# Rotation products of an SSM state stage that read PSUM instead of a ScalarE copy in SBUF

## The chip, the cores and the metric

One Trainium2 chip, one of its cores. The metric is the device time of one execution in microseconds (us), the median of three runs. Engines are named as the profile names them: PE is TensorE, DVE is VectorE, ACT is ScalarE, POOL is GpSimd, SP issues DMAs.

## The reference

One decoding step of a four-layer trunk of width 1024, in float32. It takes 272 prompt tokens (16 learned ones and 256 given) and 8 x 4 sample tokens, 304 in all. Layers 0 and 3 mix tokens with an S5 state-space model, layer 1 with pooling, layer 2 with attention; a convolutional FFN follows each. What the change touches is the state-space mixer:

```python
    a_bar = jnp.exp(lam * dt)
    b_bar = ((a_bar - 1.0) / lam)[:, :, None] * b_mat
    bu = jnp.einsum('gpc,blgc->blgp', b_bar, ug)            # complex
    bu = bu.at[:, 0].add(a_bar * h0)
    _, h = lax.associative_scan(_ssm_combine, (a_seq, bu), axis=1)
    y = jnp.real(jnp.einsum('gcp,blgp->blgc', c_mat, h)) + d_skip * uf
    z = jax.nn.gelu(y) @ w_glu
    out = z[..., :D_MODEL] * jax.nn.sigmoid(z[..., D_MODEL:])
```

## The kernel before, in words

The sequence is cut into chunks of four tokens: 68 of the prompt, 8 of the samples. Channels come in eight blocks of 128, d = 0 to 7. The complex recurrence over chunks is done in rotated coordinates, so that a real scan is enough: the inputs of the scan are multiplied by a cosine and a sine table (PT, `cs` and `sn`), scanned with the real decay R, and rotated back.

`ssm()` runs its steps in an order written as a string, `ORDER_FIRST` for layer 0 and `ORDER` for layer 3; a letter is a kind of step, the digit its block. The ones that matter here:

- i, `inputs(d)`: brings the block's tokens into the layout U by transposes on TensorE (L1062, L1067) and copies on ScalarE (u, U). In layer 3 VectorE first makes xn (L1059).
- s, `states(d)`: TensorE multiplies U by M1 (L1093), 8 small matmuls for the real part (r = 0) and 8 for the imaginary one (r = 1), each r into a PSUM bank of its own. ScalarE copies the prompt's 4 x 68 columns of a bank to E (L1095, 128x272) and the samples' 4 x 8 to Es (L1096, 128x32). VectorE then forms four products of 128x272: for each half b of the prompt E times cs (L1101) and E with r reversed times sn (L1102). One add and one subtract put them back into E (L1103, L1104). Two scans follow (L1111), the second takes over the end of the first (L1114 to L1117), then the rotation back (t3 on L1118, t4_ on L1119) and X (L1121).
- v, `outmat(d)`: GpSimd builds V from Cn and A (va on L1133, vb on L1134, then V on L1138: two instructions on VectorE for r = 0, two on GpSimd for r = 1).
- o, `outputs(d)`: TensorE multiplies U and X by m and V (L1155, L1157), ScalarE takes the GELU into z (L1159), TensorE transposes it (L1163), and ScalarE and VectorE split it into a high and a low part (zhi L1166, zlo L1167).
- g, `glu0`: groups of the GLU's matrix product, three matmuls for each product of split numbers (L248 to L250; the one with zlo is L249). Their weights are split by ScalarE (hi, L208) and by VectorE or GpSimd (lo, L211).

PSUM has eight banks; `bank()` hands out the next one as soon as its last reader is done. A list scheduler that simulates a timeline sets each engine's order from these steps, and each engine then runs its instructions strictly in that order. Each of the engines therefore waits at its own first unready instruction.

Of the kernel before, what the change touches and what calls it, by code (L numbers as in the profile page):

```python
# [9 lines left out]
F32 = mybir.dt.float32  # L10
F32R = mybir.dt.float32r
I32 = mybir.dt.int32
AF = mybir.ActivationFunctionType
ALU = mybir.AluOpType
# [8 lines left out]
KP = NP // 4  # L23
KB = KP // 2
# [22 lines left out]
def bc(ap, pos, n):  # L47

    a = ap.unsqueeze(pos)
    shape = list(a.shape)  # L50
    shape[pos] = n
    return a.broadcast_to(shape)
# [8 lines left out]
class Trunk:  # L61
# [925 lines left out]
    def ssm(self, j, l, first):  # L987
        nc, I, O = self.nc, self.I, self.O
        v, g = nc.vector, nc.gpsimd
        with self.tc.tile_pool(name=f"ssm{l}", bufs=1) as sp:  # L990
# [89 lines left out]
            def states(d):  # L1080


                qt, i0 = d // 2, d % 2 * 4
                qs = slice(4 * d, 4 * d + 4)
                M1 = self.M1[qt]
                R, E = R2[d % 2], E2[d % 2]
                nc.scalar.activation(R[:, :, :, 1:], bc(bc(self.r4[:, qs], 2, KB), 1, 2), AF.Copy)
                for r in range(2):
                    pt = self.bank()
                    for i in range(4):  # L1090
                        for h in range(2):
                            hs = slice(h * 64, h * 64 + 64)
                            nc.tensor.matmul(pt[hs, i * NK:(i + 1) * NK], M1[hs, r, i0 + i], U[d][hs, i], start=True, stop=True)  # L1093
                    pv = pt[:, :4 * NK].rearrange("p (q k) -> p q k", k=NK)
                    nc.scalar.activation(E[:, :, r, :, 1:], pv[:, :, :KP].rearrange("p q (b k) -> p b q k", b=2), AF.Copy)  # L1095
                    nc.scalar.activation(Es[:, r, qs], pv[:, :, KP:], AF.Copy)  # L1096
                cs, sn = (bc(self.PT[qt][:, i, i0:i0 + 4], 1, 2) for i in range(2))
                t1 = sp.tile([128, 2, 2, 4, KB], F32, name="t1", tag="t1", bufs=1)
                t2 = sp.tile([128, 2, 2, 4, KB], F32, name="t2", tag="t2", bufs=1)
                for b in range(2):  # L1100
                    v.tensor_tensor(t1[:, b], E[:, b, :, :, 1:], cs, ALU.mult)  # L1101
                    v.tensor_tensor(t2[:, b], E[:, b, ::-1, :, 1:], sn, ALU.mult)  # L1102
                v.tensor_tensor(E[:, :, 0, :, 1:], t1[:, :, 0], t2[:, :, 0], ALU.add)  # L1103
                v.tensor_tensor(E[:, :, 1, :, 1:], t1[:, :, 1], t2[:, :, 1], ALU.subtract)  # L1104
                x = X[d] = X3[d % 3]
                t3 = sp.tile([128, 2, 2, 4, KB], F32, name="t3", tag="t1", bufs=1)
                t4_ = sp.tile([128, 2, 2, 4, KB], F32, name="t4_", tag="t2", bufs=1)
                e1 = sp.tile([128, 2, 2, 4], F32, name="e1", tag="e1")
                for b in range(2):
                    e = E[:, b].rearrange("p r q k -> p (r q k)")  # L1110
                    v.tensor_tensor_scan(e, R.rearrange("p r q k -> p (r q k)"), e, 0.0, ALU.mult, ALU.add)  # L1111
                    if b == 0:

                        v.tensor_tensor(e1[:, 0], E[:, 0, :, :, KB], cs[:, :, :, KB - 1], ALU.mult)  # L1114
                        v.tensor_tensor(e1[:, 1], E[:, 0, ::-1, :, KB], sn[:, :, :, KB - 1], ALU.mult)
                        v.tensor_tensor(E[:, 1, 0, :, 0], e1[:, 0, 0], e1[:, 1, 0], ALU.subtract)
                        v.tensor_tensor(E[:, 1, 1, :, 0], e1[:, 0, 1], e1[:, 1, 1], ALU.add)  # L1117
                    v.tensor_tensor(t3[:, b], E[:, b, :, :, 1:], cs, ALU.mult)  # L1118
                    v.tensor_tensor(t4_[:, b], E[:, b, ::-1, :, 1:], sn, ALU.mult)  # L1119
                for r, op in ((0, ALU.subtract), (1, ALU.add)):  # L1120
                    last_s[d] = v.tensor_tensor(x[:, r, :, 1:KP + 1].rearrange("p q (b k) -> p b q k", b=2), t3[:, :, r], t4_[:, :, r], op)  # L1121
                nc.scalar.activation(fin[:, :, 8, qs], x[:, :, :, KP], AF.Copy)
                self.behind_act = nc.scalar.activation(x[:, :, :, KP:], h0[:, :, :, qs].rearrange("p r b q -> p r q b"), AF.Copy)
# [84 lines left out]
            def lift():  # L1208
                self.cap = 1 << 30

            steps = {"i": inputs, "r": residual, "w": self.ssm_w, "m": self.ssm_m, "k": self.ssm_k, "p": lambda q: self.ssm_phase(*((0, 1, v), (1, 1, g), (2, 2, g))[q]), "t": taps,
                     "s": states, "v": outmat, "o": outputs, "g": glu0, "c": self.ssm_c, "h": first_states, "L": self.consts_load,
                     "F": self.consts_finish, "C": lift, "X": self.tmp.close}
            zhi = zlo = fin = tail = None
# [516 lines left out]
```

## Time and profile before

| | us |
|---|---|
| median of three runs | 1642.25 (1640.73 to 1642.58) |
| profiled execution, its own time | 1636.96 |
| profiled execution, span from first to last instruction | 1635.3 |
| PE busy | 1482.1 (91%) |
| DVE busy | 1214.7 (74%) |
| ACT busy | 835.4 (51%) |
| POOL busy | 543.9 (33%) |

Layer 0's state stage lies between 41 and 150 us, layer 3's between 1272 and 1355 us. Busy shares over the whole span mix stages that have different limits, so a stage is read by itself: from its stretch in the table of stretches, from the chain of waits, and from the timelines of its engines. In a timeline the number in brackets is the idle time ahead of an instruction, and after the arrow stands the instruction that ended it.

### The profile page before, as it was taken

The page shows a single profiled execution, that of the slowest core. Times are in us where ns is not written, and L with a number is a line of the kernel's source. Part 1 is how long each engine was busy: PE and PEld are TensorE (multiplying, and loading weights), DVE is VectorE, ACT ScalarE, POOL GpSimd, SP SyncE. Part 2 cuts the span into 40 slices and gives each one's busy share as a digit, 9 for nine tenths or more (in the row PEclk, how much of TensorE's full clock was granted, in tenths as well). Part 3 has the DMA queues.
Part 4 walks back from the last instruction along what each step waited for, and adds up shares of the span by engine and source line. Part 5 has one row for each costly group of instructions (what it writes and reads, how often), then busy time and mean ns, then how long its engine had stood idle before and what let it go on. Part 6 is the DMA issues. An engine that isn't in the chain of part 4 may idle for free.

```text
span 1635.3 us, 31426 instructions
## 1 busy us (share of the span) xinstructions
PE 1482.1 (91%) x11272; PEld 1372.5 (84%) x11272; DVE 1214.7 (74%) x2529; ACT 835.4 (51%) x1501; POOL 543.9 (33%) x986
## 2 busy tenths in 40 slices
PE   3476999999889999999999979999977678999997
PEld 3376999999889999999665549999977678999997
DVE  7977589985689995654566646999876895799943
ACT  5463466654356663434455535666434333666643
POOL 7945045532256440100000001454193342144400
PEclk9988999999999999999999999999989799999999
DMA  6123555565335555555988895555524113455551
GB/s 115 15 48 120 158 148 158 155 188 169 105 92 155 157 161 166 168 174 196 327 315 328 308 329 147 155 157 162 173 79 113 32 31 120 138 162 167 156 173 47
DMA packets 220960, 256.24 MB, mean 157 GB/s; under 512 B 59045, under 2 KB 171861, under 8 KB 220720
## 3 DMA queue, kind: packets, MB, share of 16 engines
q1 hardware_dynamic: 218292, 249.15, 49.5%
q0 software_dynamic: 2368, 5.08, 0.9%
q8 instruction: 89, 1.46, 0.4%
q14 instruction: 67, 0.55, 0.1%
q10 hardware_dynamic: 144, 0.01, 0.0%
HBM read 246.78 MB, written 6.43 MB: 155 GB/s over the span
## 4 chain that ended last, share of the span: by engine, by line
PE 60%; DVE 8%; POOL 2%; DMA 1%; issue 1%; ACT 1%; SPq 0%; DVEq 0%; ACTq 0%; POOLq 0%
PE bk L248 16%; PE bk L250 16%; PE bk L249 16%; PE bk L1336 4%; PE zs L1356 2%; PE av L1420 2%; DVE lo L211 1%; DVE t L1102 1%; DVE E L1111 1%; DMA raw<-in_attn_w_o 1%; DVE s L648 1%; DVE t L1101 1%; PE bk L1482 0%; DVE t L1118 0%; DVE X L1121 0%
## 5 line engine op out<-in xcount | busy, mean ns | idle before, releaser
L208 ACT ACTIVATE hi<-raw 128x1024 fp32r<-128x1024 f32 x328 | 344.0, 1056 | 283.1 <-PE bk L249 237.5
L249 PE MATMUL bk<-ulo,hi 128*128 128x304 f32 (+1 forms) x1600 | 482.4, 302 | 4.1 <-DVE ulo L375 4.1
L248 PE MATMUL bk<-uhi,hi 128*128 128x304 f32 (+1 forms) x1600 | 477.6, 302 | 7.0 <-ACT uhi L374 6.8
L250 PE MATMUL bk<-uhi,lo 128*128 128x304 f32 (+1 forms) x1600 | 482.9, 302 | 0.0
L211 DVE TENSOR_TENSOR lo<-raw,hi 128x1024 fp32r<-128x1024 f32 x304 | 374.4, 1237 | 141.4 <-ACT hi L208 140.9
L249 PEld LDWEIGHTS bk<-ulo,hi 128*128 128x128 f32 x1600 | 302.4, 189 | 5.9 <-DVE ulo L375 5.1
L248 PEld LDWEIGHTS bk<-uhi,hi 128*128 128x128 f32 x1600 | 299.8, 189 | 8.6 <-ACT uhi L374 8.2
L250 PEld LDWEIGHTS bk<-uhi,lo 128*128 128x128 f32 x1600 | 301.8, 189 | 1.1 <-issue 0.4
L248 PE MATMUL bk<-ghi,hi 128*128 128x304 f32 (+1 forms) x704 | 213.1, 303 | 3.6 <-DVE so L531 3.1
L249 PE MATMUL bk<-glo,hi 128*128 128x304 f32 (+1 forms) x704 | 212.2, 302 | 0.0
L250 PE MATMUL bk<-ghi,lo 128*128 128x304 f32 (+1 forms) x704 | 210.9, 301 | 0.0
L467 ACT ACTIVATE c<-hx,cpT 128x320 f32<-128x320 f32 (+1 forms) x176 | 113.0, 645 | 94.0 <-DVE hx L461 91.4
L211 POOL TENSOR_TENSOR lo<-raw,hi 128x1024 fp32r<-128x1024 f32 x24 | 58.0, 2419 | 276.8 <-DMA raw<-in_ffn_w_up 218.3
L459 POOL COPY hx<-stT 128x16 f32<-128x16 f32 x176 | 91.2, 522 | 159.2 <-DVE c L469 154.2
L248 PEld LDWEIGHTS bk<-ghi,hi 128*128 128x128 f32 x704 | 132.7, 188 | 5.3 <-DVE so L531 4.5
L249 PEld LDWEIGHTS bk<-glo,hi 128*128 128x128 f32 x704 | 132.8, 189 | 0.1
L250 PEld LDWEIGHTS bk<-ghi,lo 128*128 128x128 f32 x704 | 132.7, 189 | 0.0
L464 POOL COPY hp<-hx 128x2 f32<-128x2 f32 x176 | 94.3, 536 | 105.3 <-DVE hx L460 98.8
L460 DVE TENSOR_TENSOR hx<-bk,rstd 128x272 f32<-128x272 f32 (+1 forms) x176 | 76.1, 433 | 31.5 <-PE bk L250 26.7
L469 DVE SCALAR_TENSOR_TENSOR c<-hx,cpT,c 128x320 f32<-128x320 f32 (+1 forms) x176 | 94.7, 540 | 1.1
L468 DVE SCALAR_TENSOR_TENSOR c<-hx,cpT,c 128x320 f32<-128x320 f32 (+1 forms) x176 | 94.5, 539 | 1.0 <-ACT c L467 0.9
L249 PE MATMUL bk<-zlo,hi 128*128 128x304 f32 (+1 forms) x256 | 77.4, 305 | 5.8 <-DVE zlo L1167 5.8
(490 smaller groups left out, 2664.8 us busy)
## 6 DMA issues: line engine op xcount, KB each, us to landing
raw<-in_ffn_w_up SPq DMA_DIRECT2D x352, 256.0 KB
raw<-in_ffn_w_down SPq DMA_DIRECT2D x88, 512.0 KB
rawx<-in_cache_v SPq DMA_DIRECT2D x38, 512.0 KB
raw<-in_cache_k SPq DMA_DIRECT2D x35, 512.0 KB
raw<-in_ssm_w_glu SPq DMA_DIRECT2D x64, 256.0 KB
rawx<-in_cache_k SPq DMA_DIRECT2D x29, 512.0 KB
raw<-in_cache_v SPq DMA_DIRECT2D x26, 512.0 KB
raw<-in_attn_w_qkv SPq DMA_DIRECT2D x24, 512.0 KB
```

Of the source, the lines that this page charges most:

```text
L208: nc.scalar.activation(hi, raw, AF.Copy)
L211: eng.tensor_tensor(lo, raw, hi.bitcast(F32), ALU.subtract)
L248: mm(out, whi, ahi, start=start, stop=False)
L249: mm(out, whi, alo, start=False, stop=False)
L250: mm(out, wlo, ahi, start=False, stop=stop)
L459: nc.gpsimd.tensor_copy(hv[:, :, 0:2], stT[:, ft].rearrange("p (b t) -> p b t", t=2))
L460: nc.vector.tensor_tensor(h[:, 2 + t0:2 + NP], ps[:, t0:NP], self.rstd[:, t0:NP], ALU.mult)
L464: nc.gpsimd.tensor_copy(hp[:, ft], h[:, NP:NP + 2])
L467: nc.scalar.activation(o, h[:, 2 + t1:], AF.Identity, bias=par(3, ft), scale=par(2, ft))
L468: nc.vector.scalar_tensor_tensor(o, h[:, 1 + t1:HEXT - 1], par(1, ft), o, ALU.mult, ALU.add)
L469: nc.vector.scalar_tensor_tensor(o, h[:, t1:HEXT - 2], par(0, ft), o, ALU.mult, ALU.add)
L1336: nc.tensor.transpose(pt[:, r * 256 + g * 128:r * 256 + (g + 1) * 128], raw[2 * s + g][:, d * 128:(d + 1) * 128], self.ident)
```

## The change

E is no longer filled by ScalarE. As soon as one r's matmuls are done, VectorE multiplies its bank directly by cs into t1[:, :, r] and by sn into t2[:, :, 1 - r], both halves b in one instruction. There are still four products of 272 columns in each state step, 64 in all; each has one input in PSUM and one in SBUF. The 32 ScalarE copies of 128x272 are gone. The copy to Es stays on ScalarE and stands after the two products of its bank. From L1102 on, lines after the change are one less than before.

```diff
@@ -1084,6 +1084,9 @@
                 qs = slice(4 * d, 4 * d + 4)
                 M1 = self.M1[qt]
                 R, E = R2[d % 2], E2[d % 2]
+                cs, sn = (bc(self.PT[qt][:, i, i0:i0 + 4], 1, 2) for i in range(2))
+                t1 = sp.tile([128, 2, 2, 4, KB], F32, name="t1", tag="t1", bufs=1)
+                t2 = sp.tile([128, 2, 2, 4, KB], F32, name="t2", tag="t2", bufs=1)
                 nc.scalar.activation(R[:, :, :, 1:], bc(bc(self.r4[:, qs], 2, KB), 1, 2), AF.Copy)
                 for r in range(2):
                     pt = self.bank()
@@ -1092,14 +1095,10 @@
                             hs = slice(h * 64, h * 64 + 64)
                             nc.tensor.matmul(pt[hs, i * NK:(i + 1) * NK], M1[hs, r, i0 + i], U[d][hs, i], start=True, stop=True)
                     pv = pt[:, :4 * NK].rearrange("p (q k) -> p q k", k=NK)
-                    nc.scalar.activation(E[:, :, r, :, 1:], pv[:, :, :KP].rearrange("p q (b k) -> p b q k", b=2), AF.Copy)
+                    e = pv[:, :, :KP].rearrange("p q (b k) -> p b q k", b=2)
+                    v.tensor_tensor(t1[:, :, r], e, cs, ALU.mult)
+                    v.tensor_tensor(t2[:, :, 1 - r], e, sn, ALU.mult)
                     nc.scalar.activation(Es[:, r, qs], pv[:, :, KP:], AF.Copy)
-                cs, sn = (bc(self.PT[qt][:, i, i0:i0 + 4], 1, 2) for i in range(2))
-                t1 = sp.tile([128, 2, 2, 4, KB], F32, name="t1", tag="t1", bufs=1)
-                t2 = sp.tile([128, 2, 2, 4, KB], F32, name="t2", tag="t2", bufs=1)
-                for b in range(2):
-                    v.tensor_tensor(t1[:, b], E[:, b, :, :, 1:], cs, ALU.mult)
-                    v.tensor_tensor(t2[:, b], E[:, b, ::-1, :, 1:], sn, ALU.mult)
                 v.tensor_tensor(E[:, :, 0, :, 1:], t1[:, :, 0], t2[:, :, 0], ALU.add)
                 v.tensor_tensor(E[:, :, 1, :, 1:], t1[:, :, 1], t2[:, :, 1], ALU.subtract)
                 x = X[d] = X3[d % 3]
```

The order of the instructions moves with it. VectorE in layer 3, from the products of step 4 (d = 4) on (E, t, e: the step's own buffers; PT: the tables; R: the decay; bk: a bank). Before:

```order
L1101 TENSOR_TENSOR t_16121<-E_15635,PT 128x272 [waits DVE_49,Activation_49]
L1102 TENSOR_TENSOR t_16122<-E_15635,PT 128x272
L1101 TENSOR_TENSOR t_16121<-E_15635,PT 128x272
L1102 TENSOR_TENSOR t_16122<-E_15635,PT 128x272
L1167 TENSOR_TENSOR zlo<-bk,zhi 128x304 [waits Activation_49]
L1103 TENSOR_TENSOR E_15635<-t_16121,t_16122 128x2x4x34 [waits DVE_49]
L1104 TENSOR_TENSOR E_15635<-t_16121,t_16122 128x2x4x34
L1111 SCALAR_TENSOR_TENSOR E_15635<-R_15633,E_15635 128x280 [waits DVE_49]
L1114 TENSOR_TENSOR e_16131<-E_15635,PT 128x8 [waits DVE_49]
L1115 TENSOR_TENSOR e_16131<-E_15635,PT 128x8
L1118 TENSOR_TENSOR t_16129<-E_15635,PT 128x272
```

After:

```order
L1099 TENSOR_TENSOR t_16074<-bk,PT 128x2x136 [waits DVE_49,PE_49]
L1100 TENSOR_TENSOR t_16075<-bk,PT 128x2x136
L1099 TENSOR_TENSOR t_16074<-bk,PT 128x2x136 [waits PE_49]
L1100 TENSOR_TENSOR t_16075<-bk,PT 128x2x136
L1103 TENSOR_TENSOR E_15619<-t_16074,t_16075 128x2x4x34 [waits DVE_49]
L1102 TENSOR_TENSOR E_15619<-t_16074,t_16075 128x2x4x34 [waits DVE_49]
L1110 SCALAR_TENSOR_TENSOR E_15619<-R_15617,E_15619 128x280 [waits DVE_49]
L1113 TENSOR_TENSOR e_16105<-E_15619,PT 128x8 [waits DVE_49]
L1114 TENSOR_TENSOR e_16105<-E_15619,PT 128x8
L1117 TENSOR_TENSOR t_16103<-E_15619,PT 128x272
L1118 TENSOR_TENSOR t__16104<-E_15619,PT 128x272
L1166 TENSOR_TENSOR zlo<-bk,zhi 128x304 [waits Activation_49]
```

The products wait for PE, each r by itself, and the zlo of the output step has moved from right behind the products to behind the first t3 and t4_ (L1117 and L1118).

ScalarE in layer 3, around the same place (U and bk: the inputs; E and Es: step 4's copies; fin and X: the end of step 3; z and zhi: the output step). Before:

```order
L1072 ACTIVATE U<-bk 128x304 [waits PE_49]
L1095 ACTIVATE E_15635<-bk 128x2x4x34 [waits PE_49]
L1096 ACTIVATE Es<-bk 128x32
L1087 ACTIVATE R_15634<-r_14694 128x8x34 [waits DVE_49]
L1095 ACTIVATE E_15635<-bk 128x2x4x34 [waits PE_49]
L1096 ACTIVATE Es<-bk 128x32
L1122 ACTIVATE fin__15701<-X_15630 128x2x4 [waits DVE_49]
L1123 ACTIVATE X_15630<-h_15659 128x8x8 [waits Activation_49]
L1159 ACTIVATE z<-bk 76x512 [waits PE_49]
L1166 ACTIVATE zhi<-bk 128x304 [waits PE_49]
```

After:

```order
L1090 ACTIVATE R_15618<-r_14678 128x8x34 [waits DVE_49]
L208 ACTIVATE hi<-raw 128x1024 [waits PE_49]
L1072 ACTIVATE U<-bk 128x304 [waits PE_49]
L1121 ACTIVATE fin__15685<-X_15614 128x2x4 [waits DVE_49]
L1122 ACTIVATE X_15614<-h_15643 128x8x8 [waits Activation_49]
L1101 ACTIVATE Es<-bk 128x32 [waits DVE_49,PE_49]
L1158 ACTIVATE z<-bk 76x512 [waits PE_49]
L1101 ACTIVATE Es<-bk 128x32 [waits DVE_49]
L1165 ACTIVATE zhi<-bk 128x304 [waits PE_49]
```

Both copies E are gone. The two Es stood ahead of fin and X and waited for PE alone; now each waits for VectorE's products of step 4, and they stand directly ahead of z and of zhi.

## Rows read from the trace of the kernel before

**Rows 1.** Table of stretches, layer 0: span, busy time per engine (instructions), granted clock, DMA.

```profile
55.40:105.00 49.60, 30.13 (x272) 28.30 (x273) 48.64 (x96) 20.58 (x64) 36.00 (x55) 0.83 0.09 16
```

**Rows 2.** Chain of waits, 1272 to 1355 us, shares by engine and line.

```profile
by line: DVE t L1102 15.0%; DVE E L1111 13.1%; DVE t L1101 11.0%; DVE t L1118 7.4%; DVE X L1121 7.3%; DVE E L1104 6.6%; issue 6.1%; DVE V L1138 5.9%; DVE E L1103 5.3%; DVE lo L211 4.8%; DVE zlo L1167 3.0%; DVE xn L1059 2.6%; DVE e L1114 1.7
```

**Rows 3.** Timeline, VectorE, layer 3 step 0: start, duration, operation, [idle before, releaser].

```profile
1272.32 0.44 DVE L1101 TENSOR_TENSOR t<-E,PT 128x272 f32<-128x272 f32 x1 [4.43 <-ACT E L1095]
...
1273.38 0.43 DVE L1102 TENSOR_TENSOR t<-E,PT 128x272 f32<-128x272 f32 x1
...
1273.73 0.53 DVE L1059 SCALAR_TENSOR_TENSOR xn<-xT,gT,rstd 128x304 f32<-128x304 f32 x1
```

**Rows 4.** Timeline, VectorE and GpSimd, layer 3 step 3.

```profile
1301.22 0.86 DVE L1102 TENSOR_TENSOR t<-E,PT 128x272 f32<-128x272 f32 x1
...
1303.67 0.47 DVE L1167 TENSOR_TENSOR zlo<-bk,zhi 128x304 fp32r<-128x304 f32 x1
...
1302.64 1.71 POOL L1138 TENSOR_TENSOR V<-va,vb 64x256 f32<-64x256 f32 x2
```

**Rows 5.** Groups by line, VectorE, layer 3 steps 1 to 7: busy us, mean ns.

```profile
L1102 DVE TENSOR_TENSOR t<-E,PT 128x272 f32<-128x272 f32 x14 | 12.8, 911 | 0.0
...
L1101 DVE TENSOR_TENSOR t<-E,PT 128x272 f32<-128x272 f32 x14 | 9.3, 666 | 0.2
```

**Rows 6.** Groups by line, VectorE, layer 0, all eight steps.

```profile
L1102 DVE TENSOR_TENSOR t<-E,PT 128x272 f32<-128x272 f32 x16 | 13.2, 828 | 0.0
L1101 DVE TENSOR_TENSOR t<-E,PT 128x272 f32<-128x272 f32 x16 | 9.8, 620 | 7.0 <-ACT E L1095 6.8
```

**Rows 7.** All instructions of one line, the FFN's L460: duration ns min/median/max.

```profile
L460 DVE TENSOR_TENSOR hx<-bk,rstd x176: 411/433/443, 214.7 to 1550.2; 128x272 f32<-128x272 f32 x132, 128x258 f32<-128x258 f32 x44
```

**Rows 8.** Timeline, ScalarE, VectorE, TensorE in turn, layer 3 step 4.

```profile
1311.95 0.57 ACT L1159 ACTIVATE z<-bk 76x512 f32<-76x512 f32 x1
...
1312.25 0.44 DVE L1101 TENSOR_TENSOR t<-E,PT 128x272 f32<-128x272 f32 x1
...
1315.05 0.46 DVE L1167 TENSOR_TENSOR zlo<-bk,zhi 128x304 fp32r<-128x304 f32 x1
1315.43 0.58 DVE L1103 TENSOR_TENSOR E<-t,t 128x272 f32<-128x272 f32 x1
...
1318.78 0.16 DVE L1116 TENSOR_TENSOR E<-e 128x4 f32<-128x4 f32 x1
...
1322.23 0.44 DVE L1101 TENSOR_TENSOR t<-E,PT 128x272 f32<-128x272 f32 x1
...
1312.58 0.48 PE L1163 MATMUL bk<-ident,z 76*128 76x76 f32 x4 [1.46 <-ACT z L1159]
...
1315.56 0.61 PE L249 MATMUL bk<-zlo,hi 128*128 128x290 f32 x1 [1.19 <-DVE zlo L1167]
...
1318.30 2.29 PE L1093 MATMUL bk<-U,M 64*64 64x76 f32 x32
1320.53 0.71 PE L1155 MATMUL bk<-m,U 128*76 128x128 f32 x2
...
1321.67 0.38 PE L1155 MATMUL bk<-m,U 128*76 128x128 f32 x2
```

**Rows 9.** Timeline, layer 0: VectorE in steps 5 and 7, GpSimd in step 7.

```profile
115.28 0.44 DVE L1101 TENSOR_TENSOR t<-E,PT 128x272 f32<-128x272 f32 x1 [6.85 <-ACT E L1095]
...
135.28 2.59 DVE L1102 TENSOR_TENSOR t<-E,PT 128x272 f32<-128x272 f32 x1
...
135.02 2.55 POOL L211 TENSOR_TENSOR lo<-raw,hi 128x1024 fp32r<-128x1024 f32 x1
```

**Rows 10.** Timeline, ScalarE, layer 3 step 0.

```profile
1271.89 0.40 ACT L1095 ACTIVATE E<-bk 128x272 f32<-128x272 f32 x1 [0.53 <-PE bk L1093]
```

**Rows 11.** All instructions of one line, the sample copy.

```profile
L1096 ACT ACTIVATE Es<-bk x32: 188/192/232, 33.4 to 1334.6; 128x32 f32<-128x32 f32 x32
```

**Rows 12.** Table of stretches, layer 3 steps 4 and 5; the clock follows POOL busy.

```profile
1312.00:1322.00 10.00, 8.16 (x65) 7.37 (x66) 9.78 (x22) 3.75 (x12) 4.75 (x6) 0.66 0.09 32
1322.00:1332.00 10.00, 8.86 (x97) 7.95 (x95) 9.78 (x22) 3.98 (x13) 4.76 (x6) 1.00 0.17 16
```

## Prediction

> **What bounds the kernel now.** The page lists TensorE as the busiest engine, but the change touches 16 state steps (eight in layer 0, eight in layer 3), so I read those stretches alone. I began with the table of stretches: in layer 0, from 55.4 to 105 us, VectorE is busy 48.64 of 49.60 us and TensorE 30.13 [rows 1]. The chain of waits for 1272 to 1355 us, which is layer 3's state stage, runs almost only over VectorE, and the four products are its largest part: 15.0% on L1102 and 11.0% on L1101 [rows 2]. (The chain view stops at 441 us, so layer 0 rests on VectorE's busy share.) So what shortens or lengthens VectorE's own instructions counts here, and a ScalarE copy counts only where VectorE stands still for it.
>
> Next, why the products cost so much. In layer 3's first step GpSimd is idle, and a product of 128x272 takes 0.43 to 0.44 us; the four go from 1272.32 to 1273.73, 1.4 us in all [rows 3]. Three steps later the same instruction takes 0.86 while GpSimd builds V. In the same stretch `zlo`, larger (304 columns) but with one input in PSUM, takes 0.47, and it lies inside GpSimd's 1.71 us on V [rows 4]. That is the argument for a gain: beside a working GpSimd, two SBUF inputs cost VectorE double, one does not.
>
> **What the change does, part by part.**
>
> *Products, contended steps.* In layer 3, from step 1 on, 28 products are busy 12.8 + 9.3 = 22.1 us [rows 5]; at 0.43 they would be 12.0, an excess of 10.1. In layer 0, 32 products take 13.2 + 9.8 = 23.0 us [rows 6], against 13.8, an excess of 9.2. The new products have one PSUM input and keep their number and size. The nearest row for their price is the FFN's L460, PSUM and SBUF, mostly 128x272: median 433 ns, maximum 443 [rows 7]. I take 0.43 for each, no dearer than an uncontended SBUF product. The bound the other way is to read `zlo`'s 0.47 as the price: 64 x 0.04 = 2.6 us given back.
>
> [...]
>
> *What of the excess only moves.* GpSimd has the same V to build, and starts on it as the products start. What now falls beside it is the two adds into E and the first scan, which still read two SBUF operands. They are already partly slow (the first add takes 0.58 in step 4 [rows 8]); I charge 0.3 us a step, 7 x 0.3 = 2 us in layer 3, and take off a third in layer 0's steps 1 to 4, where GpSimd has parameter work all through. Their excess is about 5.0 us of the 9.2, so -3.5. Step 6 gives -1.4. In step 7 one product takes 2.59 behind a 2.55 us weight split on GpSimd [rows 9]; that block then hits the next add instead, so I count -1.4 like any other step.
>
> *The ScalarE copies.* 32 copies go. VectorE stood still for them twice: layer 0's step 5 [rows 9] and layer 3's step 0. There the second copy starts at 1271.89 and the products 0.43 later [rows 10]; with each r apart, the first r's pair (0.70) is also done before. 0.43 + 0.70 = 1.1; I take -1.0, and -0.8 in layer 0. Elsewhere the copies were hidden behind VectorE, which is the cover: nothing. If that cover went, their worth would be the same 1.1 a step.
>
> *What is added: waits.* A bank is now held until VectorE's two products, and the sample copy Es, which waits for them, are done. On ScalarE the Es copies stand directly ahead of `z` and `zhi`, and on VectorE `zlo` has moved from ahead of the adds to behind the first t3/t4. Behind Es queue `z`, `zhi`, `u`, U; behind `z` TensorE's L1163, behind `zlo` TensorE's L249. Priced in step 4 of layer 3 [rows 8]: the step starts at 1312.25, and `z` started 0.30 before. With Es after the second product (0.72 on) and 0.19 long [rows 11] `z` is about 1.2 late. `zlo` started 2.80 after the step's start. Behind 1.4 of products, and the 3.35 from the first add (1315.43) to the end of t4_ (1318.78), it starts 4.8 after, 5.1 with the 0.3 above. [...]
>
> *Sum against the profiled run's 1636.96 us:* layer 3: -10.1 - 1.0 + 2 + 2 = -7.1. Layer 0: -3.5 - 0.8 - 1.4 - 1.4 = -7.1. Together -14.2, which gives 1622.8. The profiled run lies 5.3 us under the median of the runs; the difference goes on the median: 1642.25 - 14.2 = **1628.0**. Behind both stages TensorE is the bound, and starts that much earlier. Ahead of layer 0's step 5, GpSimd's weight split now stands before V, which brings it forward, and two of ScalarE's before `zhi`, which holds `zhi` back; the start of the first FFN is ordered a little differently too. The signs are mixed and no row decides them: nothing, plus or minus 2 us.
>
> **Rivals.**
>
> *A, the forecast:* 1628, its own range 1621 to 1635. For it: [rows 2 to 7].
>
> *B, TensorE's loop takes over in layer 3.* The wait for `zlo` costs every step from 3 on what the products save. Layer 3 then gives -1.0 and little more; with layer 0's -7.1 that is about -8: 1634, and 1637 if layer 0 gives only 4. [...] Against it: full clock in 1322 to 1332, with 8.86 of 10 us busy [rows 12].
>
> *C, the contention only moves.* GpSimd's work is then paid by adds and scans in full, and the two copies alone are saved: -2, 1640. For it: step 7's 2.59, which a 2.55 block sets. Against it: in step 4 [rows 8] the operations behind the first add run beside GpSimd only in part.
>
> [...]
>
> *E, more.* All excess goes and nothing is given back: -10.1 - 9.2 - 1.8 = -21: 1621 and, with the 2 us of the order, 1619.
>
> That the change does not do what it says is ruled out: in the new order the products read a bank and wait for TensorE, not ScalarE.
>
> **How the numbers follow.** A 0.60, B 0.18, C 0.09, D 0.07, E 0.06. A measurement of this kernel tells 0.2%, 3.3 us, from no change. A, B and E are faster: 0.84. C is within it: 0.09. D is slower: 0.07. The range goes from E's end to B's, each widened by 1 us for the spread of the three runs (1.9 us): 1618 to 1638. Outside it lie C and D, 0.16, and some of the edges.
>
> **What would show it.** Right: the products (now L1099 and L1100) at 0.42 to 0.48 in all 16 steps, whatever GpSimd does; L1102, L1103 and the first scan dearer by some 0.3 a step; layer 3's steps at about 8.9 us where they were 10.0; VectorE no longer waiting ahead of layer 3's first step. [...] B would show as VectorE waiting for TensorE's L1096 ahead of the products, D as the same with a granted clock near 0.5 over the whole of 1300 to 1350 us. C would show as products at 0.43 and steps as long as before.

## The result, and the profile after

The changed kernel takes 1620.82 us, the median of four runs (1618.35 to 1625.13), beside 1641.49 us, the median of four runs, for the kernel before. The ratio estimated from these runs is 0.9888, 95% interval 0.9873 to 0.9903: 18.4 us less, with 16 to 21 in the interval. The two medians lie 20.7 us apart. The profiled execution took 1621.21 us. The first lines of its page, its span and busy times:

```profile
span 1619.5 us, 31417 instructions
...
PE 1476.5 (91%) x11272; PEld 1367.5 (84%) x11272; DVE 1198.5 (74%) x2529; ACT 827.5 (51%) x1469; POOL 542.6 (34%) x986
```

VectorE lost 16.2 us of busy time (1214.7 before), ScalarE 7.9 (835.4), TensorE 5.6 (1482.1).

All instructions of the two product lines, with minimum, median and maximum in ns:

```profile
L1099 DVE TENSOR_TENSOR t<-bk,PT x32: 423/432/442, 43.8 to 1329.8; 128x272 f32<-128x272 f32 x32
```

```profile
L1100 DVE TENSOR_TENSOR t<-bk,PT x32: 423/430/432, 44.5 to 1330.2; 128x272 f32<-128x272 f32 x32
```

Against [rows 5] and [rows 6] nothing is left of the double durations: all 64 products lie between 423 and 442 ns, whatever GpSimd does beside them. They stand at the same 0.43 as the uncontended products of before in [rows 3] and as L460 in [rows 7].

Where the time came from is read from VectorE's timeline, by stage: layer 0 from the first product to the first gate of the GLU (L1182 before), layer 3 from its first xn to the first gate. Stretches outside the two stages run the same code, and the long one between them took 1101.8 to 1106.1 us in the profiles of this study, with no relation to the edits that can be seen. The first product of layer 0 comes 41.3 to 44.0 us into the span, in the trace of after 2.0 later than in that of before; so layer 3's first xn came only 8.2 us earlier, and this is the 8.2 that some expectations below give for layer 0. So the stages tell more than the whole span of one profile. The last column is the length of one state step of layer 3, from the start of step 4 to that of step 5.

| kernel | layer 0 | layer 3 | step 4 to 5 | ratio to before (95%) |
|---|---|---|---|---|
| before | 119.0 | 100.6 | 9.98 | 1 |
| after | 108.6 | 93.4 | 9.19 | 0.9888 (0.9873, 0.9903) |
| after again (e10) | 108.4 | 93.6 | 9.20 | 0.9890 (0.9871, 0.9908) |
| e1, copy and SBUF | 118.1 | 100.7 | 9.99 | 0.9990 (0.9977, 1.0003) |
| e2, copy and PSUM | 108.5 | 93.6 | 8.94 | 0.9900 (0.9883, 0.9918) |
| e3, layer 0 only | 111.9 | 101.7 | 10.00 | 0.9950 (0.9933, 0.9968) |
| e4, layer 3 only | 119.5 | 93.3 | 9.19 | 0.9944 (0.9925, 0.9964) |
| e5, before, GpSimd idle in layer 3 | 119.5 | 88.9 | 7.71 | 0.9914 (0.9894, 0.9934) |
| e6, after, GpSimd idle in layer 3 | 111.9 | 86.7 | 7.68 | 0.9839 (0.9820, 0.9858) |
| e7, adds from PSUM | 111.6 | 91.9 | 8.49 | 0.9897 (0.9881, 0.9913) |
| e8, Es behind the adds | 104.1 | 86.8 | 8.73 | 0.9828 (0.9808, 0.9848) |
| e9, R in PSUM | 102.0 | 91.4 | 8.42 | 0.9816 (0.9794, 0.9837) |

In these two traces layer 3 gave 7.2 us and layer 0 10.4 (7.1 to 11.1 with other traces, below).

What the products saved did not all arrive. VectorE's groups by line over steps 1 to 7 of layer 3, busy us and mean ns of one, before:

```profile
L1111 DVE TENSOR_TENSOR_SCAN E<-R,E 128x280 f32<-128x280 f32 x14 | 11.0, 784 | 0.3
...
L1104 DVE TENSOR_TENSOR E<-t,t 128x272 f32<-128x272 f32 x7 | 5.6, 794 | 0.0
L1103 DVE TENSOR_TENSOR E<-t,t 128x272 f32<-128x272 f32 x7 | 5.0, 716 | 0.2
...
L1114 DVE TENSOR_TENSOR e<-E,PT 128x8 f32<-128x8 f32 x7 | 1.2, 172 | 0.2
L1115 DVE TENSOR_TENSOR e<-E,PT 128x8 f32<-128x8 f32 x7 | 1.2, 165 | 0.0
```

and after:

```profile
L1110 DVE TENSOR_TENSOR_SCAN E<-R,E 128x280 f32<-128x280 f32 x14 | 12.2, 870 | 0.4
...
L1102 DVE TENSOR_TENSOR E<-t,t 128x272 f32<-128x272 f32 x7 | 6.1, 872 | 0.0
L1099 DVE TENSOR_TENSOR t<-bk,PT 128x272 f32<-128x272 f32 x14 | 6.1, 435 | 0.2
L1100 DVE TENSOR_TENSOR t<-bk,PT 128x272 f32<-128x272 f32 x14 | 6.0, 430 | 0.0
L1103 DVE TENSOR_TENSOR E<-t,t 128x272 f32<-128x272 f32 x7 | 5.6, 806 | 0.0
...
L1113 DVE TENSOR_TENSOR e<-E,PT 128x8 f32<-128x8 f32 x7 | 2.1, 306 | 0.2
...
L1114 DVE TENSOR_TENSOR e<-E,PT 128x8 f32<-128x8 f32 x7 | 1.6, 224 | 0.0
```

The products fell from the 22.1 us of [rows 5] to 6.1 + 6.0. The adds rose from 10.6 to 11.7, the scans from 11.0 to 12.2, the two small e products behind the first scan from 2.4 to 3.7: 3.6 us over seven steps went to the instructions that now run beside GpSimd, 0.5 us a step.

Step 4 of layer 3 after the change, VectorE, to be laid beside [rows 8]:

```profile
1300.34 0.43 DVE L1099 TENSOR_TENSOR t<-bk,PT 128x272 f32<-128x272 f32 x1
...
1301.39 0.43 DVE L1100 TENSOR_TENSOR t<-bk,PT 128x272 f32<-128x272 f32 x1
1301.74 0.84 DVE L1103 TENSOR_TENSOR E<-t,t 128x272 f32<-128x272 f32 x1
1302.50 0.96 DVE L1102 TENSOR_TENSOR E<-t,t 128x272 f32<-128x272 f32 x1
1303.50 1.04 DVE L1110 TENSOR_TENSOR_SCAN E<-R,E 128x280 f32<-128x280 f32 x1
...
1305.69 0.46 DVE L1166 TENSOR_TENSOR zlo<-bk,zhi 128x304 fp32r<-128x304 f32 x1
...
1309.53 0.44 DVE L1099 TENSOR_TENSOR t<-bk,PT 128x272 f32<-128x272 f32 x1
```

The products end 1.4 us after the start; both adds (0.84 and 0.96) and the scan (1.04) are slow; `zlo` starts 5.35 us after the step's start, where it started 2.80 after; and the next step starts without a wait. ScalarE and TensorE in the same step:

```profile
1301.22 0.20 ACT L1101 ACTIVATE Es<-bk 128x32 f32<-128x32 f32 x1 [2.22 <-DVE t L1100]
1301.31 0.58 ACT L1158 ACTIVATE z<-bk 76x512 f32<-76x512 f32 x1
```

```profile
1303.97 1.27 PE L1096 MATMUL bk<-U,M 64*64 64x76 f32 x32
...
1308.81 0.38 PE L249 MATMUL bk<-zlo,hi 128*128 128x290 f32 x1
```

`z` starts 0.97 after the step's start, behind Es, where it started 0.30 ahead. TensorE runs the next step's matmuls (L1096) at 1303.97, ahead of the GLU's L249 that needs `zlo`; in [rows 8] L249 stood ahead of them.

### The profile page after: what moved, and what is told of

It is laid out like the page before. It is cut to its first block, busy times and chain, and to the rows that moved or that the text cites. A ratio compares the mean times of both kernels' runs of the same rounds, so it can differ in the third digit from the quotient of the medians.

```text
span 1619.5 us, 31417 instructions
## 1 busy us (share of the span) xinstructions
PE 1476.5 (91%) x11272; PEld 1367.5 (84%) x11272; DVE 1198.5 (74%) x2529; ACT 827.5 (51%) x1469; POOL 542.6 (34%) x986
## 4 chain that ended last, share of the span: by engine, by line
PE 62%; DVE 7%; POOL 2%; ACT 1%; issue 1%; DMA 0%; SPq 0%; DVEq 0%; ACTq 0%; POOLq 0%
PE bk L248 16%; PE bk L250 16%; PE bk L249 16%; PE bk L1335 4%; PE zs L1355 2%; PE av L1419 2%; DVE lo L211 1%; DVE E L1110 1%; DVE s L648 1%; PE bk L1481 1%; DMA rawx<-in_cache_v 0%; DVE ulo L375 0%; PE bk L940 0%; PE bk L1156 0%; DVE X L1120 0%
## 5 line engine op out<-in xcount | busy, mean ns | idle before, releaser
L249 PE MATMUL bk<-ulo,hi 128*128 128x304 f32 (+1 forms) x1600 | 482.1, 302 | 4.2 <-DVE ulo L375 4.2
L249 PEld LDWEIGHTS bk<-ulo,hi 128*128 128x128 f32 x1600 | 302.5, 189 | 5.9 <-DVE ulo L375 5.2
L249 PE MATMUL bk<-glo,hi 128*128 128x304 f32 (+1 forms) x704 | 212.3, 302 | 0.0
L249 PEld LDWEIGHTS bk<-glo,hi 128*128 128x128 f32 x704 | 132.8, 189 | 0.1
L460 DVE TENSOR_TENSOR hx<-bk,rstd 128x272 f32<-128x272 f32 (+1 forms) x176 | 76.2, 433 | 35.5 <-PE bk L250 30.4
L249 PE MATMUL bk<-zlo,hi 128*128 128x304 f32 (+1 forms) x256 | 76.7, 303 | 2.6 <-DVE zlo L1166 2.6
```

The lines of the kernel that those rows point to most:

```text
L249: mm(out, whi, alo, start=False, stop=False)
L460: nc.vector.tensor_tensor(h[:, 2 + t0:2 + NP], ps[:, t0:NP], self.rstd[:, t0:NP], ALU.mult)
```

## Experiments

**The source, or the arrangement (e1, e2).** The first run keeps the arrangement of the change and puts back the ScalarE copy and the SBUF source:

```diff
+                    nc.scalar.activation(E[:, :, r, :, 1:], pv[:, :, :KP].rearrange("p q (b k) -> p b q k", b=2), AF.Copy)
-                    e = pv[:, :, :KP].rearrange("p q (b k) -> p b q k", b=2)
+                    e = E[:, :, r, :, 1:]
```

> The change without its main point: ScalarE copies E as before, the products are arranged as after (each r by itself, both halves in one instruction) but read E in SBUF. Theory (the gain is the second SBUF operand beside a working GpSimd): products at about 0.86 us in contended steps, 22 us of product time in layer 3's steps 1 to 7 as before, time within 3 us of before, 1638 to 1643. Rival (the gain comes from the new arrangement and order): products may stay slow but the time falls by 10 us or more.

Measured: 1639.16 us against 1640.84, ratio 0.9990 (0.9977 to 1.0003), both stages as before. The sine products read, as all instructions of one line:

```profile
L1101 DVE TENSOR_TENSOR t<-E,PT x32: 430/860/2582, 44.5 to 1347.1; 128x272 f32<-128x272 f32 x32
```

A median of 860 ns: with the second operand back in SBUF the doubling is back (22.6 us of products in steps 1 to 7 of layer 3, 22.1 before), and with it the time. The arrangement alone (each r apart, both halves in one instruction) gives nothing that can be measured.

The second run keeps the PSUM source and adds the copy as dead work ahead of the products:

```diff
+                    nc.scalar.activation(E[:, :, r, :, 1:], pv[:, :, :KP].rearrange("p q (b k) -> p b q k", b=2), AF.Copy)
                     e = pv[:, :, :KP].rearrange("p q (b k) -> p b q k", b=2)
```

> The changed kernel with the ScalarE copies put back as dead work ahead of the products: the products read PSUM as after, but start behind the copy. Theory: products at 0.43 everywhere, and of the gain of about 18 us only the two places where VectorE stood still for the copy are lost, 2 to 3 us, so 1623 to 1628. Rival (the gain is ScalarE's freed time and the shorter way from TensorE to VectorE): the gain goes, 1636 or more.

Measured: 1623.41 us, ratio 0.9900 (0.9883 to 0.9918), not to be told from the change itself. The products stay at 0.43, and the first of layer 3 waits for the copy:

```profile
L1101 DVE TENSOR_TENSOR t<-bk,PT x32: 425/431/431, 43.1 to 1329.3; 128x272 f32<-128x272 f32 x32
```

```profile
1253.20 1.79 DVE L1059 SCALAR_TENSOR_TENSOR xn<-xT,gT,rstd 128x304 f32<-128x304 f32 x2
...
1261.74 0.44 DVE L1100 TENSOR_TENSOR t<-bk,PT 128x272 f32<-128x272 f32 x1 [3.42 <-ACT E L1098]
```

From the first xn to the first product it takes 8.54 us, against 8.11 after the change (1254.57 to 1262.68) and 9.56 before. So one copy costs 0.43 there, as counted, but the stage is as long as after (93.6 and 93.4): the 2 to 3 us that were expected to be lost were not. The 32 copies as such were worth nothing that these runs can show. The two runs together settle it: the gain is the source of the operand.

**By layer (e3, e4).** Each applies the change in one layer and leaves the other as before (the edit in outline):

```diff
+                if first:        # e3; "not first" in e4
+                    ...          # the products from PSUM
+                else:
+                    ...          # copies and products from SBUF
```

> The change in layer 0's state stage alone. By the two traces of before and after layer 0 gave 8.2 us and layer 3 7.2 us. Theory: about 8 us below before, 1632 to 1635, and layer 3's stage as before (steps of 10.0 us). Rival (the two are not independent, layer 3's order depends on what comes before): the sum of the two single-layer gains misses the whole by more than 4 us.

> The change in layer 3's state stage alone. Theory: about 7 us below before, 1633 to 1636, layer 0's stage as before. Rival: as for the layer 0 run, the two gains do not add up.

Measured: 0.9950 and 0.9944 of before, about 8 and 9 us; 1633.0 and 1632.53 us. The sum, 17.4 us, is within 1 us of the whole (18.4). By the medians it is 16.2 against 20.7; each ratio is known to some 3 us, so the runs agree with two gains that add up, but can't tell 1 us from 4. The stages agree better: e3 has layer 3 nearly as before (101.7, step 4 of 10.0), e4 has layer 0 as before (119.5) and layer 3 as after (93.3).

**GpSimd taken away (e5, e6).** From block 2 on in layer 3, GpSimd computes no va, vb and V; VectorE keeps its half, with block 1's va and vb. Done to the kernel before and to the changed one:

```diff
+                    if not first and d >= 2:
+                        if r:
+                            continue
+                        a, b = self.va0, self.vb0
+                    else:
                         ...
```

> The kernel before, with GpSimd's part of V (va, vb and its half of V) left out in layer 3 from block 2 on; VectorE's half of V reads block 1's va and vb again, so V is wrong there. Theory: with GpSimd idle the SBUF products fall to 0.43 us by themselves, adds and scans too, and layer 3's steps 2 to 6 take about 8 us where they took 10 to 11. Together with the next run: the pair differs by about 10 us (layer 0's 8.2, step 0's 1.7 and part of step 1), not by 18. Rival (the gain is in the order or in ScalarE's copies): the pair still differs by 15 us or more.

> The changed kernel with the same GpSimd work left out in layer 3 from block 2 on. Theory: steps 2 to 6 of layer 3 as long as in the run before it, to 0.2 us each, since nothing is left that the PSUM source could save; adds at 0.43 and first scans at 0.74, which shows the 0.5 us a step that the change only moved. Rival: steps shorter than that run's by the 0.8 us of the real pair.

VectorE in one step of the first (start of the step, add, scan, start of the next):

```profile
1312.26 0.44 DVE L1101 TENSOR_TENSOR t<-E,PT 128x272 f32<-128x272 f32 x1
...
1314.06 0.43 DVE L1103 TENSOR_TENSOR E<-t,t 128x272 f32<-128x272 f32 x1
...
1314.88 0.74 DVE L1111 TENSOR_TENSOR_SCAN E<-R,E 128x280 f32<-128x280 f32 x1
...
1319.97 0.44 DVE L1101 TENSOR_TENSOR t<-E,PT 128x272 f32<-128x272 f32 x1
```

and of the second:

```profile
1305.99 0.43 DVE L1099 TENSOR_TENSOR t<-bk,PT 128x272 f32<-128x272 f32 x1
...
1307.38 0.43 DVE L1103 TENSOR_TENSOR E<-t,t 128x272 f32<-128x272 f32 x1
...
1308.20 0.74 DVE L1110 TENSOR_TENSOR_SCAN E<-R,E 128x280 f32<-128x280 f32 x1
...
1313.67 0.44 DVE L1099 TENSOR_TENSOR t<-bk,PT 128x272 f32<-128x272 f32 x1
```

Now the SBUF products, adds and scans of before run at 0.43 to 0.44, 0.43 and 0.74 too, and step 4 takes 7.71 and 7.68 us in the two kernels. Over the whole stage the pair differs by 2.1 us instead of 7.2, and 1.4 of that is the start of the first step (9.44 against 8.00 from the first xn). The two whole runs differ by 11.7 us (1628.17 and 1616.45); 7.5 of it is layer 0, where GpSimd keeps its work in both. In steps 1 to 6 of before no wait of VectorE for GpSimd shows, so what left with GpSimd's work is not a wait but the longer durations. It shows the cause, and the size of what is left: step 4 took 9.98 with GpSimd's work before and 9.19 after, 7.7 without it. Of the 2.3 us that GpSimd's presence cost there, the change took off 0.8.

Not all steps did what was expected. Steps 2, 3 and 6 of the pair differ by 0.4 to 0.6 us, and not all the same way. Step 3 did not get shorter at all: 11.89 and 12.31 us, where before took 11.39. In it VectorE waits 2.23 and 2.92 us for `zhi`. In the second kernel TensorE's granted clock was 0.56 in the step 2 ahead of it; that the clock is the reason was not tested.

**One step further (e7, e8, e9).** If the adds are the next to pay, they can be fed from PSUM too: the cosine product goes back into its own bank.

```diff
...
-                    v.tensor_tensor(t1[:, :, r], e, cs, ALU.mult)
                     v.tensor_tensor(t2[:, :, 1 - r], e, sn, ALU.mult)
+                    v.tensor_tensor(e, e, cs, ALU.mult)
+                    c1.append(e)
...
-                v.tensor_tensor(E[:, :, 0, :, 1:], t1[:, :, 0], t2[:, :, 0], ALU.add)
-                v.tensor_tensor(E[:, :, 1, :, 1:], t1[:, :, 1], t2[:, :, 1], ALU.subtract)
+                v.tensor_tensor(E[:, :, 0, :, 1:], c1[0], t2[:, :, 0], ALU.add)
+                v.tensor_tensor(E[:, :, 1, :, 1:], c1[1], t2[:, :, 1], ALU.subtract)
```

> The changed kernel, one step further: the cosine product is written back in place into its PSUM bank, so each add into E has one PSUM and one SBUF input too. Theory: the adds, 0.81 to 0.87 us in layer 3, fall to 0.43 to 0.45; part of the contention moves on to the first scan and the e1 products behind it, so 0.4 us a step remain: 3 us in layer 3 and as much in layer 0, 1613 to 1617. Rival (it all moves on, or the bank held longer stops TensorE): 1619 to 1624.

Measured: 1623.42 us, ratio 0.9897 (0.9881 to 0.9913): no gain over the change. A miss, though the adds did get faster: scans and adds by line, steps 1 to 7 of layer 3, and below them VectorE's waits ahead of the adds (us in total, times, longest):

```profile
L1111 DVE TENSOR_TENSOR_SCAN E<-R,E 128x280 f32<-128x280 f32 x14 | 12.5, 890 | 0.4
...
L1104 DVE TENSOR_TENSOR E<-bk,t 128x272 f32<-128x272 f32 x7 | 3.1, 436 | 1.3 <-ACT Es L1102 1.3
L1103 DVE TENSOR_TENSOR E<-bk,t 128x272 f32<-128x272 f32 x7 | 3.0, 434 | 1.0 <-ACT Es L1102 1.0
```

```profile
DVE E L1104 <- ACT Es L1102: 1.3, 1, 1.3
...
DVE E L1103 <- ACT Es L1102: 1.0, 1, 1.0
```

The adds fell to 0.43, and steps 4 and 5 to 8.5 us. But steps 2 and 3 did not get shorter: here an add waits for Es. Both read the same bank, the program had Es ahead of the adds, and Es stands behind `z` on ScalarE, which waits for TensorE. That is not the whole miss: layer 3's stage is still 1.5 us shorter than after the change, and layer 0's is 3.0 longer (111.6 against 108.6). There Es holds the adds for 0.8 us only; a wait of 2.50 for a DMA (m from kq) and one of 2.75 for `zhi` stand beside it, and what they owe to the edit is open. Next, the copies to Es were moved behind the adds:

```diff
...
-                    nc.scalar.activation(Es[:, r, qs], pv[:, :, KP:], AF.Copy)
+                    c2.append(pv)
...
+                for r in range(2):
+                    nc.scalar.activation(Es[:, r, qs], c2[r][:, :, KP:], AF.Copy)
```

> The kernel with adds fed from PSUM, with the copies to Es moved behind the adds, so that VectorE's adds no longer wait for ScalarE's Es (1.28 and 0.97 us in the trace of the run without this). Theory: layer 3's steps 4 and 5 stay at 8.5 us, steps 2 and 3 lose these waits, the stage from its first xn to its first gate is 1.5 to 2.5 us shorter than 91.9; 1615 to 1621. Rival (Es and z later still, TensorE's output groups come to bound the steps): as long as the run before, 1621 to 1626.

Measured: 1611.82 us (1610.3 to 1616.7), ratio 0.9828 (0.9808 to 0.9848), about 10 us below the change and better than was expected. VectorE's longest waits in the stage:

```profile
DVE t L1099 <- PE bk L1096: 3.2, 2, 3.0
DVE zlo L1169 <- ACT zhi L1168: 2.3, 2, 2.1
```

None is left ahead of the adds. From step 0 to step 7 the stage is 3.1 us shorter than after the change (63.35 against 66.46), and its tail, from step 7 to the first gate, another 3.5 (15.3 against 18.85); layer 0 is 4.5 shorter. Of the tail's gain 2.9 is VectorE's wait for `zhi` there, 2.1 instead of 5.0. The order of the instructions moved as well, so the gain can't be put down to the place of Es alone. Last, ScalarE writes the decay R to a PSUM bank, so that the scan has one SBUF operand too:

```diff
-                R, E = R2[d % 2], E2[d % 2]
+                E = E2[d % 2]
+                R = self.bank()[:, :8 * (KB + 1)].rearrange("p (r q k) -> p r q k", r=2, q=4)
+                nc.scalar.activation(R[:, :, :, :1], bc(bc(self.r4[:, qs], 2, 1), 1, 2), AF.Copy, scale=0.0)
```

> The kernel before this, with the decay R also put in a PSUM bank by ScalarE, so that the scan too has one SBUF input. Theory: the first scan falls from 1.04 to 0.74 in contended steps, part of it moves on to t3 and t4_; 1 to 2 us less in each layer: 1612 to 1619. Rival (a bank more per step starves TensorE of banks, or ScalarE's longer work for R shows): slower than the run before by 2 us or more.

```profile
L1115 DVE TENSOR_TENSOR_SCAN E<-bk,E 128x280 f32<-128x280 f32 x14 | 10.3, 739 | 0.8
```

The scans fell to 0.74 from a mean of 0.93 in the run before, and layer 0 to 102.0. In layer 3 the steps 1 to 5 are 1.4 us shorter than in e8, but step 6 is 1.7 longer and the tail 4.3 (19.6 us from step 7 to the first gate), and the whole, 1610.85 us and 0.9816 (0.9794 to 0.9837), can't be told from e8.

**The change again (e10).** Beside e8 and e9, on the same chip:

> The changed kernel once more, beside the two above on one chip, for a comparison in the same runs. Theory: 0.986 to 0.991 of before, 1618 to 1627. A second point: its layer 0 had 18.6 us from step 4 to step 5, two other kernels with the same order there 21.7 at a granted clock of 0.5; the profile shows which is the rule.

1622.63 us against 1642.31, ratio 0.9890 (0.9871 to 0.9908). Its layer 0 had 18.5 us from step 4 to step 5; what that says is in the last section.

## Why the prediction was right, and where it was off

Forecast 1628.0 with 1618 to 1638; measured 1620.82. Direction and mechanism held, and the size was short: 14.2 us against 18.4 by the ratio. The measured time lies just below the forecast's own range (1621 to 1635) and at the number of rival E (1621); it is inside the stated range because that was drawn out to E's end. E's mechanism is not what happened: it wanted nothing given back, and 3.6 us were in layer 3. The sum for layer 3 came out, 7.1 us forecast and 7.2 measured, but by luck: two wrong terms in it cancel, as the points below show. The shortfall lies in layer 0.

**Price of a PSUM operand: right.** 0.43 was taken from L460 [rows 7], and 423 to 442 ns was measured. The end at `zlo`'s 0.47 was not reached. The products from PSUM took 0.42 to 0.44 us, the uncontended ones from SBUF 0.43 to 0.44 [rows 3]: a bank as the source made none dearer.

**Contention as the cause: right, and shown.** The excess of 10.1 us in layer 3 was to go; 22.1 became 12.1. e1 brings it back by the source alone, e5 removes it by GpSimd alone.

**What only moves: too low in layer 3, too high in layer 0.** 0.3 us a step was charged, 0.5 measured, 3.6 us in layer 3 instead of 2. The first of the adds was seen to be partly slow already; the e products behind the scan were left out of the list. In layer 0 the terms leave 2.9 of the excess of 9.2 to be paid elsewhere (and a third off 5.0 is 3.3, not 3.5). In sum nothing of it shows. Over the stage VectorE's busy time fell by 9.4, from 100.24 before to 90.89 after (columns as in [rows 1]):

```profile
41.83:160.83 119.00, 74.91 (x681) 69.55 (x682) 100.24 (x198) 54.62 (x153) 77.66 (x107) 0.89 0.24 62
```

```profile
43.82:152.44 108.62, 72.92 (x679) 67.25 (x680) 90.89 (x198) 52.68 (x144) 76.32 (x107) 0.83 0.26 69
```

Step 7 of layer 0 shows one reason. The weight split that held a product for 2.59 us [rows 9] now holds an add, for 1.83, as described. But a second split held step 7's first scan before, for 2.83 (at 139.69), and that scan now takes 0.74. Against it stands a new wait of 2.70 for ScalarE's `hi` ahead of the step.

**The ScalarE copies: right in place, small in size.** The first product of layer 3 comes 1.45 us earlier, where 1.0 was counted. e2 shows that the copy's own part is 0.43 and that it doesn't reach the end. The 0.8 of layer 0 can't be read: the wait ahead of step 5 was 5.3 to 6.9 us in the three traces with the old stage (before, e4, e5) and 4.3 to 6.7 in four with the new one (after, e3, e6, e10).

**The wait for `zlo`: a step that failed.** `z` was to come about 1.2 us late and came 1.27 late; `zlo` was to start 5.1 us into the step and started 5.35. Both were right, but not the 2 us that the sum for layer 3 adds for waits. They are the author's estimate that VectorE would stand still for the next step's bank in one and a half of steps 3 to 7, at a low granted clock, and no run shows the term. The estimate took TensorE's order from the trace of before, L249 ahead of the next step's matmuls. In the new program they stand the other way round, and the trace shows it: L1096 at 1303.97, L249 at 1308.81, products at 1309.53 with no wait. VectorE waits for L1096 in layer 3 only in step 0 (3.0 and 0.2 us). So the 2 us charged, and rivals B and D with it, fell. The order was not the only condition that failed: the granted clock was 1.00 in each of steps 3 to 6, where the stretch of before that the estimate was read from had 0.66 [rows 12]. No run separates the two. The table of stretches (columns as in [rows 1]) shows steps 4 and 5:

```profile
1300.30:1309.50 9.20, 6.97 (x82) 6.22 (x81) 9.01 (x22) 3.24 (x9) 4.44 (x6) 1.00 0.19 59
1309.50:1318.80 9.30, 7.13 (x82) 6.38 (x81) 9.08 (x21) 3.24 (x9) 4.47 (x6) 1.00 0.18 18
```

The order of TensorE could have been read from the new program, as that of VectorE and ScalarE was.

**Layer 0 by its stage: short by up to 4 us.** 7.1 was counted. The stage took 119.0 to 119.5 us in before, e4 and e5, 108.6 and 108.4 in after and e10, and 111.9 in e3 and e6, where the granted clock stood at 0.50 for some 10 us of step 4 to 5 (last section). So the change took off 10.4 to 11.1 us in the first two and 7.1 to 7.6 in the other two; that the latter meet the 7.1 is chance, since VectorE's busy time fell by more than 9 us in e3 too (90.90) and more waiting made up for it.

With 3.6 in the place of 2, 1.45 in the place of 1.0 and nothing for the wait, layer 3's sum is -10.0 - 1.45 + 3.6 = -7.9, measured -7.2. Layers 3 and 0 together give 14.3 to 18.3 by their stages, and 18.4 by the ratio. The rest, up to 4 us, is no larger than what the same code between the layers varies by, and stays open.

## What to carry to other kernels

Where VectorE and GpSimd work side by side, look at VectorE's two-operand instructions one by one: here the same instruction at 0.43 and at 0.86 in different steps meant that GpSimd worked beside an instruction with two SBUF operands, and one operand left in PSUM ended that at no cost that could be measured. Then ask what runs in the shadow next: the instructions that follow inherit the neighbour (0.5 of 1.4 us a step in layer 3), and feeding them from PSUM too paid in e8, not in e7, where VectorE was made to wait for another reader of the same bank. And where an edit moves the schedule, read the order of every engine in the chain that is priced, not of the two that are most in view.

## What was not expected of the hardware

The same order of instructions ran layer 0's step 4 to 5 in 18.6, 18.5, 21.7 and 21.7 us (after, e10, e3, e6). The columns are span, busy time of PE, PEld, DVE, ACT and POOL, then the granted clock, the DMA share and GB/s. After:

```profile
97.00:102.00 5.00, 2.34 (x21) 2.11 (x20) 4.82 (x16) 1.34 (x4) 1.47 (x2) 0.94 0.25 58
102.00:107.00 5.00, 5.00 (x32) 4.55 (x31) 1.38 (x5) 4.91 (x12) 4.58 (x5) 0.72 0.24 25
107.00:112.00 5.00, 5.00 (x67) 4.74 (x66) 0.74 (x3) 3.71 (x12) 3.89 (x4) 1.00 0.37 72
```

e3, which has the same layer 0:

```profile
97.00:102.00 5.00, 2.33 (x22) 2.10 (x21) 4.79 (x15) 1.67 (x5) 1.13 (x2) 0.97 0.18 37
102.00:107.00 5.00, 5.00 (x24) 4.55 (x23) 0.72 (x2) 4.89 (x11) 4.91 (x5) 0.50 0.28 38
107.00:112.00 5.00, 5.00 (x25) 4.97 (x26) 0.58 (x2) 2.14 (x8) 3.53 (x3) 0.51 0.32 57
```

e10:

```profile
97.00:102.00 5.00, 3.97 (x38) 3.74 (x38) 4.83 (x15) 1.74 (x4) 1.93 (x3) 1.00 0.40 110
102.00:107.00 5.00, 5.00 (x40) 4.54 (x39) 2.01 (x6) 4.89 (x11) 4.19 (x4) 1.00 0.28 28
107.00:112.00 5.00, 4.70 (x63) 4.13 (x61) 0.98 (x3) 4.37 (x16) 4.30 (x5) 1.00 0.39 76
```

In e3 the granted clock stood at 0.50 and 0.51 for 10 us, while TensorE was busy throughout; in e10 it stayed at 1.00, in after it was 0.72 for 5 us and 1.00 for the next 5. In the 5 us ahead TensorE was busy for 2.33 and 2.34 us in e3 and after, for 3.97 in e10 (layer 0's first product came within 0.3 us of the same time in all three). So one and the same order of instructions took 3 us longer in the traces where the clock stood at 0.50. After and e3 had nearly the same busy time ahead, and the outcome still differed; what decides it was not settled.
